# Last feed-forward stage: the weights' high part meets both halves of x in one 512-column matmul

## The chip, the core and the metric

The kernel runs on one core of a Trainium2 chip. Its engines are TensorE (PE, with its weight loads shown as PEld), VectorE (DVE), ScalarE (ACT), GpSimd (POOL) and SyncE (SP), which issues the transfers. The metric is the device time of one execution in microseconds (us), lower is better.

## The reference

Two blocks of two layers each follow each other on a sequence of 256 tokens of width 1024. The first block has three kinds of attention and a mixture of experts, the second puts 16 meta tokens in front (272 in all) and has a delta-rule mixer in its first layer, dense attention in its second, each with a feed-forward after it. The change is in the very last feed-forward:

```python
u = rmsnorm(h, mlp_norm_g[layer])
h = h + jnp.square(jax.nn.relu(u @ w_ff1[layer])) @ w_ff2[layer]
return h[:, N_META:]
```

`w_ff1` is 1024 x 4096, `w_ff2` 4096 x 1024. Everything is float32. In this last layer the meta tokens are no longer needed, so the stage works on 256 columns (tokens), the same stage of the layer before on 272.

## The kernel before

**Numbers in two parts.** PE multiplies in a fast format (fp32r) that keeps fewer bits, so each operand a is split into a high part, a rounded to that format, and a low part, a - high. `wsplit` (lines 256 and 267 for the subtraction) splits 128 x 1024 weights: ACT converts the high part (line 236, out `ring`), DVE subtracts (line 267). `split` does the same for a result (ACT, then DVE at line 249). `mm3` forms a product as three matmuls into one bank: high weights with high x (line 272), high weights with low x (273), low weights with high x (274). Each matmul instruction has its own weight load. `form_a` does this for the eight slices of 128 of a contraction of 1024, one slice being called a k-step here: 24 matmuls per block of 128 output features.

**The stage.** `mlp(l, lo, out)` is called with `lo=16` for the last layer, so n = 256. Its input u is h2 times the norm's gain, in two parts; the norm's factor per token (`rs`) is put on the way out of the first product. The hidden width of 4096 is worked through in four quarters. In each, ff1 makes eight blocks: 24 matmuls into a bank, then on DVE `max(b, 0) * rs` into `fr` (line 245), its square on POOL (line 1299), and the split into rh (ACT) and rl (DVE). Then ff2 makes eight blocks of the 1024 output features from the quarter's rh and rl, the first two of them side by side k-step by k-step, and DVE adds each to the residual h2 (`add_h`, line 1269). In the last quarter `leave` sends two features blocks of h2 out at a time. So the stage has 32 blocks of ff1 and 32 of ff2.

**What sets the order.** The tile framework turns the program into one queue per engine and puts in the semaphores; each engine then works through its queue in order, and that order need not be the one in which the code writes the instructions. Split weights lie in two pairs of buffers in turn (`NW = 2`), so the split of block i+2 may begin when block i has been multiplied; the second block of the side-by-side pair takes a ring slot instead (`spare`). There are four banks for such products, and two buffers each of rh, rl and fr. Weights come in from SP's queue in transfers of 1 MB into ring slots. `norm_start(i, lo)` prepares u for the next stage one feature block at a time as h2 gets its last addend: ACT writes uh, DVE ul (line 245), ACT and POOL sum the squares; i = 3 is the norm ahead of this stage, called by the output projection of the attention (`out_proj`).

Of the kernel before, what the change touches and what calls it, by code (L numbers as in the profile page):

```python
# [10 lines left out]
F32R = mybir.dt.float32r  # L11
# [14 lines left out]
N2 = S + 16  # L26
# [154 lines left out]
class Kern:  # L181
# [11 lines left out]
    def bank(self, tag="bank"):  # L193
        return self.ps.tile([128, 512], F32, name=tag, bufs=BANKS[tag])
# [1026 lines left out]
    def hcols(self, t):  # L1221
        return slice(0, 16) if t == 0 else slice(16 + 128 * (t - 1), 144 + 128 * (t - 1))

    def norm_tiles(self, n):

        uh, ul = (self.hp.tile([128, 8, N2], F32R, name=m)[:, :, :n] for m in ("uh", "ul"))
        acc = self.hp.tile([128, N2], F32, name="acc")[:, :n]

        def scale():
            ss = self.aux()[:, :n]  # L1230
            self.nc.tensor.matmul(ss, self.ones, acc, start=True, stop=True)
            rs = self.hp.tile([128, N2], F32, name="nrs")[:, :n]
            self.rstd(rs, ss, D, self.eps6)
            return rs

        self.norm = (uh, ul), scale
        return uh, ul, acc

    def square(self, acc, x, k):
# [5 lines left out]
            self.nc.gpsimd.tensor_add(acc, acc, sq)  # L1245

    def norm_start(self, i, lo=0):
        uh, ul, acc = self.norm_tiles(N2 - lo)

        def step(k):  # L1250
            x, g = self.h2[:, k, lo:], self.g2[:, i, k:k + 1]
            self.act(uh[:, k], x, AF.Copy, scale=g)
            self.stt(ul[:, k], x, g, uh[:, k].bitcast(F32), OP.mult, OP.subtract)
            self.square(acc, x, k)

        return step
# [10 lines left out]
    def add_h(self, k, b, lo=0, then=None):  # L1267
        n = N2 - lo
        self.nc.vector.tensor_add(self.h2[:, k, lo:], self.h2[:, k, lo:], b[:, :n])  # L1269
        if then is not None:  # L1270
            then(k)

    def mlp(self, l, lo=0, out=None):
        nc, a, tc = self.nc, self.a, self.tc
        n = N2 - lo
        then = None

        def leave(k):
            if k % 2:
                nc.sync.dma_start(out[:, k - 1:k + 1], self.h2[:, k - 1:k + 1, 16:])  # L1280

        with ExitStack() as c:
            p2 = c.enter_context(tc.tile_pool(name=f"Fw{l}", bufs=2))
            u, scale = self.norm
            rs = None
            for q in range(4):
                rh = p2.tile([128, 8, n], F32R, name="rh")
                rl = p2.tile([128, 8, n], F32R, name="rl")
                for c4 in range(2):
                    w = self.ring(a["w_ff1"][l, 2 * q + c4])  # L1290
                    for j in range(4):
                        f = 4 * c4 + j
                        b = self.bank()[:, :n]
                        self.form_a(b, w[:, j * 1024:(j + 1) * 1024], u)
                        if rs is None:
                            rs = scale()
                        r = p2.tile([128, n], F32, name="fr")
                        self.stt(r, b, 0.0, rs, OP.max, OP.mult)
                        nc.gpsimd.tensor_mul(r, r, r)  # L1299
                        self.split(rh[:, f], rl[:, f], r)  # L1300
                if q == 3:
                    then = self.norm_start(2) if out is None else leave
                for c4 in range(2):
                    w = self.ring(a["w_ff2"][l, 2 * q + c4])
                    pair = range(0 if c4 else 2)
                    if pair:
                        bs = [self.bank()[:, :n] for _ in pair]
                        parts = [self.wsplit(w[:, j * 1024:(j + 1) * 1024], spare=j == 1) for j in pair]
                        for k in range(8):
                            c = slice(k * 128, (k + 1) * 128)  # L1310
                            for b, (hi, lw) in zip(bs, parts):
                                self.mm3(b, (hi[:, c], lw[:, c]), (rh[:, k], rl[:, k]), k == 0, k == 7)
                        for j, b in enumerate(bs):
                            self.add_h(j, b, lo, then)
                    for j in range(len(pair), 4):
                        f = 4 * c4 + j
                        b = self.bank()[:, :n]
                        self.form_a(b, w[:, j * 1024:(j + 1) * 1024], (rh, rl))
                        self.add_h(f, b, lo, then)

    def conv_silu(self, p, b, rs, wc, out):

# [1027 lines left out]
```

## Time and profile before

| | |
|---|---|
| Median of three runs | 1559.42 us (1555.83 to 1578.79) |
| Profiled execution | 1559.64 us |
| Its span in the profile | 1557.9 us |
| PE, DVE, ACT, POOL busy | 95%, 53%, 41%, 11% of the span |
| First matmul of the changed stage | 1369.87 us |
| Last matmul's end | 1554.06 us |

A profile row gives an instruction's start and its duration in us, the engine, the source line, the operation, the tiles it writes and reads (out<-in), their shapes, and how many were merged; in brackets the engine's idle time before it and what ended that. Matmuls overlap: a row's duration holds the time until its results are out, and the distance from one start to the next is what a matmul takes of PE.

### The profile page before, as it was taken

To read this page: it belongs to the slowest core of one execution; us is meant where nothing else is said; L and a number is where in the kernel's file an instruction comes from. 1 tells how busy PE (TensorE), PEld (TensorE's weight loads), DVE (VectorE), ACT (ScalarE), POOL (GpSimd) and SP (SyncE) were. 2 spreads that over 40 slices of the span, in tenths; PEclk is the share of its full clock that TensorE was granted. 3 is DMA by queue.
4 is the path that set the end of the run, shared out by engine and by line. 5 is a ranking of instruction groups with operands and counts; after the bars stand their busy time and mean duration, and the time that the engine had idled before them with its cause. 6 is when DMAs were issued, how large, how long until landed. Compare 5 with 4: busy or idle time off the path is not lost.

```text
span 1557.9 us, 26416 instructions
## 1 busy us (share of the span) xinstructions
PE 1479.8 (95%) x10806; PEld 1128.8 (72%) x10806; DVE 821.7 (53%) x1594; ACT 638.1 (41%) x1265; POOL 178.2 (11%) x226
## 2 busy tenths in 40 slices
PE   8999999999799999999989888899999999999999
PEld 7888744344388874434328777679999997899998
DVE  6687712212336782222126686557556566576665
ACT  5466411111246642111125674455444455554443
POOL 0130000000001000000003530302001123221000
PEclk9999999999899999999998998799999999999999
DMA  9336799999833679999943210036454542255540
GB/s 382 121 136 222 300 417 420 383 421 423 331 134 108 222 300 391 422 383 421 422 193 120 71 54 31 1 136 243 163 184 168 190 145 84 83 196 185 179 141 28
DMA packets 50033, 348.76 MB, mean 224 GB/s; under 512 B 5616, under 2 KB 6896, under 8 KB 8688
## 3 DMA queue, kind: packets, MB, share of 16 engines
q1 hardware_dynamic: 49904, 346.97, 57.9%
q8 instruction: 89, 1.46, 0.4%
q14 instruction: 40, 0.33, 0.1%
HBM read 345.90 MB, written 1.05 MB: 223 GB/s over the span
## 4 chain that ended last, share of the span: by engine, by line
PE 43%; DVE 5%; ACT 3%; POOL 1%; issue 1%; DVEq 0%; POOLq 0%; ACTq 0%
PE bank L274 10%; PE bank L272 10%; PE bank L273 10%; PE bank L1060 3%; PE bank L1102 2%; DVE ring L267 1%; PE aux L297 1%; ACT ring L236 1%; PE aux L2059 1%; PE bank L1690 1%; PE aux L1558 1%; PE aux L2037 1%; POOL cy L1336 0%; DVE v L245 0%; PE bank L1847 0%
## 5 line engine op out<-in xcount | busy, mean ns | idle before, releaser
L236 ACT ACTIVATE ring<-ring 128x1024 fp32r<-128x1024 f32 (+4 forms) x198 | 196.2, 1001 | 211.1 <-PE bank L274 189.4
L267 DVE TENSOR_TENSOR ring<-ring,ring 128x1024 fp32r<-128x1024 f32 x162 | 202.8, 1253 | 93.8 <-ACT ring L236 93.5
L274 PE MATMUL bank<-uh,ring 128*128 128x272 f32 (+1 forms) x744 | 216.9, 292 | 7.4 <-DVE ring L267 6.0
L272 PE MATMUL bank<-uh,ring 128*128 128x272 f32 (+1 forms) x744 | 220.0, 296 | 3.3 <-ACT ring L236 3.3
L273 PE MATMUL bank<-ul,ring 128*128 128x272 f32 (+1 forms) x744 | 215.8, 290 | 0.0
L274 PEld LDWEIGHTS bank<-uh,ring 128*128 128x128 f32 x744 | 142.9, 192 | 9.4 <-DVE ring L267 7.5
L272 PEld LDWEIGHTS bank<-uh,ring 128*128 128x128 f32 x744 | 142.8, 192 | 5.4 <-ACT ring L236 4.2
L273 PEld LDWEIGHTS bank<-ul,ring 128*128 128x128 f32 x744 | 142.6, 192 | 0.6
L274 PE MATMUL bank<-rh,ring 128*128 128x272 f32 (+1 forms) x496 | 141.7, 286 | 0.0
L272 PE MATMUL bank<-rh,ring 128*128 128x272 f32 (+1 forms) x496 | 141.5, 285 | 0.0
L273 PE MATMUL bank<-rl,ring 128*128 128x272 f32 (+1 forms) x496 | 140.9, 284 | 0.0
L1073 DVE TENSOR_TENSOR hid<-hid,bank 128x512 f32<-128x512 f32 x16 | 11.0, 687 | 193.4 <-PE bank L1060 193.4
L273 PEld LDWEIGHTS bank<-rl,ring 128*128 128x128 f32 x496 | 93.8, 189 | 0.0
L272 PEld LDWEIGHTS bank<-rh,ring 128*128 128x128 f32 x496 | 93.2, 188 | 0.0
L274 PEld LDWEIGHTS bank<-rh,ring 128*128 128x128 f32 x496 | 93.0, 188 | 0.0
L245 DVE SCALAR_TENSOR_TENSOR big<-bank,gs,big 128x512 fp32r<-128x512 f32 x32 | 24.0, 751 | 108.8 <-ACT big L236 107.3
L1299 POOL TENSOR_TENSOR fr<-fr 128x272 f32<-128x272 f32 (+1 forms) x64 | 40.0, 627 | 287.5 <-DVE fr L245 283.6
L236 ACT ACTIVATE big<-bank,gs 128x512 fp32r<-128x512 f32 x32 | 22.0, 687 | 102.2 <-PE bank L1102 101.9
L1269 DVE TENSOR_TENSOR h<-h,bank 128x272 f32<-128x272 f32 (+1 forms) x80 | 33.2, 426 | 51.5 <-PE bank L274 51.5
L236 ACT ACTIVATE hid<-bank 128x512 f32<-128x512 f32 x24 | 14.3, 597 | 108.9 <-PE bank L1060 103.9
L1083 ACT COPY hidT<-bank 128x512 f32<-128x512 f32 x16 | 9.4, 586 | 118.3 <-PE bank L297 118.3
L1102 PE MATMUL bank<-big,hidT 128*64 128x512 f32 x208 | 47.8, 595 | 0.1
(668 smaller groups left out, 3391.4 us busy)
## 6 DMA issues: line engine op xcount, KB each, us to landing
ring<-w_ff SPq DMA_DIRECT2D x58, 1024.0 KB, 4.8
big<-w_gate SPq DMA_DIRECT2D x30, 1024.0 KB, 17.5
big<-w_up SPq DMA_DIRECT2D x29, 1024.0 KB, 18.1
big<-w_down SPq DMA_DIRECT2D x26, 1024.0 KB, 17.1
ring<-w_gate SPq DMA_DIRECT2D x24, 1024.0 KB, 14.1
ring<-w_down SPq DMA_DIRECT2D x24, 1024.0 KB, 17.5
ring<-w_up SPq DMA_DIRECT2D x20, 1024.0 KB, 18.1
big<-w_in SPq DMA_DIRECT2D x9, 1024.0 KB, 11.8
```

The costliest lines, as they stand in the source:

```text
L236: return self.nc.scalar.activation(out, in_, func, **kw)
L245: return (eng or self.nc.vector).scalar_tensor_tensor(out, in0, s, in1, op0=op0, op1=op1, **kw)
L267: (eng or self.nc.vector).tensor_sub(l, src, h.bitcast(F32))
L272: mm(out, lhs[0], rhs[0], start=first, stop=False)
L273: mm(out, lhs[0], rhs[1], start=False, stop=False)
L274: mm(out, lhs[1], rhs[0], start=False, stop=last)
L297: self.nc.tensor.transpose(out, in_, self.ident[:k, :k])
L1060: mm(b[e * 64:e * 64 + CAP], xg[:, k, e * CAP:(e + 1) * CAP], w[:, (2 * k + e) * 512:(2 * k + e + 1) * 512], start=k == 0, stop=k == 7)
L1102: mm(yb[n][e * 64:e * 64 + CAP], hT[:, k, e * 64:e * 64 + CAP], w[:, o:o + 512], start=k == 0, stop=k == 3)
L1269: self.nc.vector.tensor_add(self.h2[:, k, lo:], self.h2[:, k, lo:], b[:, :n])
L1299: nc.gpsimd.tensor_mul(r, r, r)
L1558: nc.tensor.matmul(ob[r, dst.start - c0:dst.stop - c0], vba[:n, u, r], x[:n, u], start=u == 0, stop=u == 2)
```

## The change

Where n is 256, u lies in one tile `uw` with both parts of a k-step side by side (256 columns high, 256 low), and so do rh and rl. A whole bank of 512 columns takes a block. A k-step is two matmuls: the high weights with all 512 columns, the low weights with the 256 high ones, into the bank's first half. The last k-step has them the other way round. On the way out the two halves are summed: in ff1 ACT copies the second half into `fr` and DVE adds the first half to it, after which `max` and `rs` are applied to `fr` in place; in ff2 DVE adds first one half and then the other to h2. The stage of 272 columns keeps the three matmuls.

```diff
--- before.py
+++ after.py
@@ -1221,9 +1221,13 @@
     def hcols(self, t):
         return slice(0, 16) if t == 0 else slice(16 + 128 * (t - 1), 144 + 128 * (t - 1))
 
-    def norm_tiles(self, n):
-
-        uh, ul = (self.hp.tile([128, 8, N2], F32R, name=m)[:, :, :n] for m in ("uh", "ul"))
+    def norm_tiles(self, n, wide=False):
+
+        if wide:
+            u = self.hp.tile([128, 8, 2, n], F32R, name="uw")
+            uh, ul = u[:, :, 0], u[:, :, 1]
+        else:
+            u = uh, ul = [self.hp.tile([128, 8, N2], F32R, name=m)[:, :, :n] for m in ("uh", "ul")]
         acc = self.hp.tile([128, N2], F32, name="acc")[:, :n]
 
         def scale():
@@ -1233,7 +1237,7 @@
             self.rstd(rs, ss, D, self.eps6)
             return rs
 
-        self.norm = (uh, ul), scale
+        self.norm = u, scale
         return uh, ul, acc
 
     def square(self, acc, x, k):
@@ -1245,7 +1249,7 @@
             self.nc.gpsimd.tensor_add(acc, acc, sq)
 
     def norm_start(self, i, lo=0):
-        uh, ul, acc = self.norm_tiles(N2 - lo)
+        uh, ul, acc = self.norm_tiles(N2 - lo, i == 3)
 
         def step(k):
             x, g = self.h2[:, k, lo:], self.g2[:, i, k:k + 1]
@@ -1270,31 +1274,66 @@
         if then is not None:
             then(k)
 
+    def wide(self, out, parts, x, k, first, last):
+
+        hi, lo = parts
+        c = slice(k * 128, (k + 1) * 128)
+        steps = [(out, hi[:, c], x[:, k]), (out[:, 0], lo[:, c], x[:, k, 0])]
+        for o, w, m in steps[::-1] if last else steps:
+            self.nc.tensor.matmul(o, w, m, start=first and o is out, stop=last and o is out)
+
     def mlp(self, l, lo=0, out=None):
         nc, a, tc = self.nc, self.a, self.tc
         n = N2 - lo
         then = None
+        both = n == 256
 
         def leave(k):
             if k % 2:
                 nc.sync.dma_start(out[:, k - 1:k + 1], self.h2[:, k - 1:k + 1, 16:])
+
+        def bank():
+            return self.bank().rearrange("p (a s) -> p a s", a=2) if both else self.bank()[:, :n]
+
+        def block(b, parts, x, k):
+            if both:
+                return self.wide(b, parts, x, k, k == 0, k == 7)
+            c = slice(k * 128, (k + 1) * 128)
+            self.mm3(b, (parts[0][:, c], parts[1][:, c]), (x[0][:, k], x[1][:, k]), k == 0, k == 7)
+
+        def add(f, b):
+            if both:
+                nc.vector.tensor_add(self.h2[:, f, lo:], self.h2[:, f, lo:], b[:, 1])
+                b = b[:, 0]
+            self.add_h(f, b, lo, then)
 
         with ExitStack() as c:
             p2 = c.enter_context(tc.tile_pool(name=f"Fw{l}", bufs=2))
             u, scale = self.norm
             rs = None
             for q in range(4):
-                rh = p2.tile([128, 8, n], F32R, name="rh")
-                rl = p2.tile([128, 8, n], F32R, name="rl")
+                if both:
+                    rt = p2.tile([128, 8, 2, n], F32R, name="rh")
+                    rh, rl = rt[:, :, 0], rt[:, :, 1]
+                else:
+                    rh = p2.tile([128, 8, n], F32R, name="rh")
+                    rl = p2.tile([128, 8, n], F32R, name="rl")
+                    rt = rh, rl
                 for c4 in range(2):
                     w = self.ring(a["w_ff1"][l, 2 * q + c4])
                     for j in range(4):
                         f = 4 * c4 + j
-                        b = self.bank()[:, :n]
-                        self.form_a(b, w[:, j * 1024:(j + 1) * 1024], u)
+                        b = bank()
+                        parts = self.wsplit(w[:, j * 1024:(j + 1) * 1024])
+                        for k in range(8):
+                            block(b, parts, u, k)
                         if rs is None:
                             rs = scale()
                         r = p2.tile([128, n], F32, name="fr")
+                        if both:
+                            nc.scalar.copy(r, b[:, 1])
+                            nc.vector.tensor_add(r, r, b[:, 0])
+                            b = r
                         self.stt(r, b, 0.0, rs, OP.max, OP.mult)
                         nc.gpsimd.tensor_mul(r, r, r)
                         self.split(rh[:, f], rl[:, f], r)
@@ -1304,19 +1343,19 @@
                     w = self.ring(a["w_ff2"][l, 2 * q + c4])
                     pair = range(0 if c4 else 2)
                     if pair:
-                        bs = [self.bank()[:, :n] for _ in pair]
+                        bs = [bank() for _ in pair]
                         parts = [self.wsplit(w[:, j * 1024:(j + 1) * 1024], spare=j == 1) for j in pair]
                         for k in range(8):
-                            c = slice(k * 128, (k + 1) * 128)
-                            for b, (hi, lw) in zip(bs, parts):
-                                self.mm3(b, (hi[:, c], lw[:, c]), (rh[:, k], rl[:, k]), k == 0, k == 7)
+                            for b, p in zip(bs, parts):
+                                block(b, p, rt, k)
                         for j, b in enumerate(bs):
-                            self.add_h(j, b, lo, then)
+                            add(j, b)
                     for j in range(len(pair), 4):
-                        f = 4 * c4 + j
-                        b = self.bank()[:, :n]
-                        self.form_a(b, w[:, j * 1024:(j + 1) * 1024], (rh, rl))
-                        self.add_h(f, b, lo, then)
+                        b = bank()
+                        parts = self.wsplit(w[:, j * 1024:(j + 1) * 1024])
+                        for k in range(8):
+                            block(b, parts, rt, k)
+                        add(4 * c4 + j, b)
 
     def conv_silu(self, p, b, rs, wc, out):
 
```

## Rows read from the trace of the kernel before

**Rows 1.** The page, part 1: busy time, share of the span, instructions.

```profile
PE 1479.8 (95%) x10806; PEld 1128.8 (72%) x10806; DVE 821.7 (53%) x1594; ACT 638.1 (41%) x1265; POOL 178.2 (11%) x226
```

**Rows 2.** Busy by stretch: us, PE, PEld, DVE, ACT, POOL (counts), PEclk, DMA share, GB/s.

```profile
1369.90:1554.10 184.20, 183.75 (x1540) 183.29 (x1538) 114.44 (x161) 80.00 (x98) 20.96 (x34) 1.00 0.41 142
...
1416.70:1439.50 22.80, 22.80 (x195) 22.80 (x194) 15.54 (x23) 11.42 (x15) 4.30 (x7) 1.00 0.55 186
```

**Rows 3.** The chain of waits, stage alone, by line.

```profile
by line: PE bank L274 32.3%; PE bank L273 32.0%; PE bank L272 31.8%; ACT ring L236 0.6%; POOL acc L1245 0.5%; PE aux L1231 0.4%; DVE h L1269 0.2%; ACT uh L236 0.2%; ACT nsq L236 0.2%; issue 0.1%; POOLq L1245 0.0%
```

**Rows 4.** Groups of instructions in the stage: busy us, mean ns | idle before.

```profile
L267 DVE TENSOR_TENSOR ring<-ring,ring 128x1024 fp32r<-128x1024 f32 x55 | 67.6, 1230 | 34.9 <-ACT ring L236 34.9
...
L245 DVE SCALAR_TENSOR_TENSOR fr<-bank,nrs 128x256 f32<-128x256 f32 x32 | 13.6, 424 | 6.2 <-PE bank L274 6.1
```

**Rows 5.** PE in order of time: first matmuls of ff1, ff2, next ff1.

```profile
1416.72 0.28 PE L272 MATMUL bank<-uh,ring 128*128 128x256 f32 x1
...
1439.41 0.28 PE L272 MATMUL bank<-rh,ring 128*128 128x256 f32 x1
...
1462.45 0.28 PE L272 MATMUL bank<-uh,ring 128*128 128x256 f32 x1
```

**Rows 6.** PE in order of time: 512-column matmuls, long run, then mixed.

```profile
148.00 0.39 PE L273 MATMUL bank<-wsp,ring 128*128 128x512 f32 x1
...
153.90 0.39 PE L272 MATMUL aux<-ring,ring 128*128 128x512 f32 x1
...
161.69 0.40 PE L272 MATMUL bank<-wsp,big 128*128 128x512 f32 x1
...
162.16 0.28 PE L273 MATMUL aux<-big,ring 128*16 128x256 f32 x1
```

**Rows 7.** PE in order of time: 272-column matmuls of the earlier stage.

```profile
1170.08 0.29 PE L272 MATMUL bank<-uh,ring 128*128 128x272 f32 x1
...
1179.92 0.29 PE L272 MATMUL bank<-uh,ring 128*128 128x272 f32 x1
```

**Rows 8.** One ff1 block's way out, by engine in order of time.

```profile
1419.52 0.28 PE L272 MATMUL bank<-uh,ring 128*128 128x256 f32 x1
...
1422.48 0.19 PEld L274 LDWEIGHTS bank<-uh,ring 128*128 128x128 f32 x1
...
1422.60 0.28 PE L274 MATMUL bank<-uh,ring 128*128 128x256 f32 x1
...
1419.72 1.06 ACT L236 ACTIVATE ring<-ring 128x1024 fp32r<-128x1024 f32 x1 [1.74 <-PE bank L274]
1420.93 0.42 ACT L236 ACTIVATE rh<-fr 128x256 fp32r<-128x256 f32 x1 [0.15 <-POOL fr L1299]
...
1419.72 0.42 DVE L245 SCALAR_TENSOR_TENSOR fr<-bank,nrs 128x256 f32<-128x256 f32 x1 [0.48 <-PE bank L274]
1420.81 1.22 DVE L267 TENSOR_TENSOR ring<-ring,ring 128x1024 fp32r<-128x1024 f32 x1 [0.67 <-ACT ring L236]
```

**Rows 9.** ACT copies out of a bank; DVE line 245 with SBUF operands.

```profile
1298.03 0.35 ACT L2052 COPY PTc<-aux 128x256 f32<-128x256 f32 x1
1298.28 0.25 ACT L2053 COPY PTc<-aux 16x128 f32<-16x128 f32 x1
...
1296.78 0.48 DVE L245 SCALAR_TENSOR_TENSOR crx<-cub,wsp,csq 128x256 f32<-128x256 f32 x1 [0.33 <-ACT csq L236]
...
1364.89 0.96 DVE L245 SCALAR_TENSOR_TENSOR ul<-h,wsp,uh 128x256 fp32r<-128x256 f32 x1
```

**Rows 10.** The first block's last k-step: DVE and PE.

```profile
1372.30 0.95 DVE L245 SCALAR_TENSOR_TENSOR ul<-h,wsp,uh 128x256 fp32r<-128x256 f32 x1
1372.34 0.28 PE L272 MATMUL bank<-uh,ring 128*128 128x256 f32 x1
```

**Rows 11.** DVE adds to h2: after a pair, and at the end.

```profile
1399.28 0.78 DVE L1269 TENSOR_TENSOR h<-h,bank 128x256 f32<-128x256 f32 x2 [2.75 <-PE bank L274]
...
1554.09 0.42 DVE L1269 TENSOR_TENSOR h<-h,bank 128x256 f32<-128x256 f32 x1 [2.45 <-PE bank L274]
```

## The prediction

> **What bounds the kernel now.** I read the page's busy shares first: PE is busy for 95% of the span [rows 1]. Then the stretches of the stage that the change touches, the last feed-forward (1369.9 to 1554.1 us): in the 22.8 us from 1416.7, which are the first half of one quarter, PE and its weight loads are both busy without a gap, the granted clock is 1.00 (the 2.4 GHz level), DVE is busy 15.54 us of 22.8, ACT 11.42 [rows 2]. The chain of waits through the stage agrees: 96% of it is lines 272 to 274, the three matmuls of a k-step [rows 3]. So the stage is a stream of matmuls, and its time is their number times the distance from one start to the next. The duration that a matmul's row shows (0.28) is longer than that distance and is not what one costs.
>
> The distance is read from starts. In the first half of a quarter (ff1) 192 matmuls of 256 columns lie between 1416.72 and 1439.41: 22.69 / 192 = 118.2 ns each. In the second half (ff2), 192 from there to 1462.45: 23.04 / 192 = 120.0 ns [rows 5]. At 2.4 GHz 256 columns stream in 106.7 ns, so each matmul costs 11.5 or 13.3 ns beside its columns. Is that a price per matmul or per column? A run of 512-column matmuls in the same number format has 26 steps from 148.00 to 153.90: 226.9 ns, 13.6 over the 213.3 of its columns [rows 6]. A run of 272 columns has 78 steps from 1170.08 to 1179.92: 126.2 ns, 12.8 over 113.3 [rows 7]. Twice the columns, the same surplus: it belongs to the matmul. This is what the change can save, and nearly all of it, because the number of columns streamed (768 per k-step) stays.
>
> **The change part by part.**
> *Products.* Of three matmuls per k-step (256 columns each) remain one of 512 and one of 256. There are 64 blocks of 8 k-steps. ff1: before 3 x 118.2 = 354.6 ns, after 226.9 + 118.2 = 345.1, saved 9.5. ff2: before 360.0, after 226.9 + 120.0 = 346.9, saved 13.1. The first ff1 block gains nothing: PE reaches its last k-step at 1372.34 and waits there for ul, which DVE ends at 1373.25 [rows 10], and the changed order waits for the same ul. So 31 x 8 x 9.5 ns = 2.4 us and 32 x 8 x 13.1 ns = 3.4 us: 5.8 us saved.
> No row shows 512 and 256 columns in turn with weights that change each time. From below: no surplus is left, 320 ns per k-step, which saves 34.6 x 248 + 40 x 256 = 8.6 + 10.2 = 18.8 us. From above: in a mixed stretch two 512-column matmuls took 235 ns each (161.69 to 162.16 for both) [rows 6], so 353.2 and 355.0 per k-step, which saves 1.4 x 248 + 5 x 256 = 1.6 us. I take the long run's 226.9, since it is 26 alike in the same place of a queue, and the mixed stretch has other products between.
>
> *Way out of ff1.* New per block: an ACT copy of the low half, a DVE add of the two halves, and the max-times-scale that reads SBUF now. DVE per block was 1.23 (low part of the weights), 0.42 and 0.42; it becomes some 2.5 us of a block of 8 x 345.1 = 2.76 us [rows 4], ACT some 1.9 (1.06, 0.42 and the new 0.36). Neither is the bound by its sum, but the order in the queues matters. Two weight pairs alternate: the high part of block i+2 can be converted on ACT only when block i has left PE, and DVE subtracts after that. Now ACT starts this conversion at 1419.72, DVE the subtraction at 1420.81 until 1422.03 [rows 8], that is 2.31 after the block's visible end T. When it is needed: the next block's first matmul starts 0.20 before T (1419.52); the block after that starts 2.76 later, its first low-part matmul 0.23 on, and that one's weight load 0.12 earlier (1422.48 against 1422.60): T + 2.67 [rows 8].
> With the change ACT gets the copy at T too. It is earlier in the program, so I expect it first. From a like copy to the next ACT start there are 0.25 us [rows 9], so the conversion runs from T + 0.27 to 1.33. DVE meanwhile adds (T + 0.39, next start 0.35 later) and scales (from 0.74); the scaling with SBUF operands took 0.48, or 0.96 beside a POOL instruction [rows 9], and POOL's square comes after it. So it is done before the subtraction, which runs from T + 1.36 to 2.58. Margin 0.06 us (it was about 0.5). I cost this way out at nothing: PE's stream hides it. If the cover is gone by x, that is lost once per two blocks (two pairs): at 0.40 for the copy, x = 0.09 and 32 x 0.045 = 1.4 us. The bound below is nothing gained, since PE did not wait there.
> Behind the copy ACT also queues the conversion of the squared result, behind the add DVE queues the rest of that block's split. Who waits for these is ff2, a k-step of which reads one feature block; the last of them is read at the end of the first pair, some 5 us later.
>
> *Way out of ff2.* A second DVE add per block (0.42, second of two 0.36 later [rows 11]). It fills the 0.67 that DVE waits for ACT ahead of a subtraction [rows 8]: the adds end at T + 0.78, the subtraction starts at T + 1.09. After the pair of blocks there are four adds instead of two, T to T + 1.44, then the subtraction to 2.66: due at 2.67 again, so nothing. At the end of the kernel nothing hides it: the last add ends at 1554.51 now [rows 11], one more costs 0.36 us, before the last output transfer.
>
> *The rest.* The normalised input lands in one fresh tile instead of two reused ones, the instructions are the same and none waits longer. The weight transfers are issued by the same rule at the same places; DMA share in the stage is 0.41 [rows 2] and the stage wants its weights 3% faster. The last k-step puts the low-part matmul ahead of the wide one, which changes no count. The other feed-forward (272 columns) takes the old path.
>
> Sum against the profiled execution of 1559.64 (span 1557.9 and 1.74 around it): 1559.64 - 5.8 + 0.36 = 1554.2 us. The median of the three runs is 1559.42, 0.2 lower, so it stands for both.
>
> [...]
>
> **The rivals.**
> A, weight loads set the pace. Loads are busy the whole stage [rows 2], and one of three goes. If the surplus comes from loads that don't quite fit beside 256 columns, under 512 they fit, and the k-step falls towards 320 ns: 1559.64 - 18.8 + 0.36 = 1541.2. Against it: 512 columns leave room for a load of 0.19 and still show 13.6 ns of surplus [rows 6]. [...]
> B, the other side: the subtraction falls behind the way out. Place: DVE's queue in each of 32 ff1 blocks. If ACT converts the weights first and copies after (T + 0.97 to 1.33) and DVE's queue has the add and the scaling ahead of the subtraction, it runs from 2.13 to 3.35, is seen at 3.38 and due at 2.67: 0.71 per two blocks, 32 x 0.355 = 11.4 us. 1554.2 + 11.4 = 1565.6, slower than before; it decides against the change once the delay passes 5.4 us / 16 = 0.34 per two blocks. For it: DVE's queue is in a fixed order, and the trace already has ACT instructions ahead of ones that the code writes earlier (the weights of block i+2 before the result of block i [rows 8]). Against it: that reordering favours the weights, on DVE too.
> C, the change doesn't do what it says: the wide matmul costs what the mixed stretch shows (235 ns). Saved 1.6, less 0.36: 1558.4. For it: only that stretch has changing shapes. Against it: its neighbours differ in output and weights' width too.
>
> **How the numbers follow.** Forecast 0.62 (own range 1552.5 to 1556.5: the copy's 1.4 us upward, 11.5 instead of 13.6 ns for ff1's wide matmul downward), A 0.10, B 0.13, C 0.15. The range 1546 to 1566 holds the forecast, C, B and the halfway part of A; what is left out is A's end, and a B with a larger delay. A change of 2% (31 us) is about what a measurement of this kernel tells from none. No case reaches 1528, since 768 columns stream in 320 ns: 0.01 for what I can't see. Slower than 1591 would need three times B's delay: 0.04. Within 2%: 0.95.
>
> **What would show it.** PE matmuls in the stage fall from 1536 to 1024, starts of a k-step are 345 to 347 ns apart, and the weight loads' busy share falls below 1. The chain stays on PE. ACT's row order in an ff1 block is copy, weights, result, and DVE's subtraction ends about 2.6 us after the block. Waits of PE on the ring's DVE subtraction, some tenths each in ff1, would show B; k-steps of 320 ns A; of 353 C. The forecast is wrong in its main step if 227 + 119 isn't what wide and narrow cost in turn.

## The result, and the profile after

The changed kernel takes 1575.59 us in the median of 22 runs (1569.41 to 1594.18), the kernel before 1563.28 in 22 runs beside it. The ratio is 1.0074, with a 95% interval of 1.0062 to 1.0087: slower by 12 us, where 5 us less were forecast. It lies within the 2% that counted as the same, and above the range given. One run of the 22, the longest, had a lower granted clock (0.92 for 0.97) and is left out of the ratio.

The profiled execution took 1577.20 us, 17.6 more than that of before. 5.0 of these lie ahead of the stage: its first matmul starts at 1374.87 instead of 1369.87. Five kernels of the experiments, whose code ahead of the stage is the changed one's, start it anywhere from 1370.30 to 1374.45, so this is a difference between executions. The stage itself, from there to the end of the last add, went from 184.64 us (1369.87 to 1554.51) to 196.89 (1374.87 to 1571.76): 12.25 more, the same as the medians say. All readings below are of the stage.

The page of the kernel after, part 1, as in [rows 1]:

```profile
PE 1488.2 (94%) x10294; PEld 1101.6 (70%) x10294; DVE 847.8 (54%) x1658; ACT 644.1 (41%) x1297; POOL 207.3 (13%) x226
```

The matmuls fell by 512, as the change says. POOL has as many instructions as before, 226, and yet is busy for 29 us more (178.2 in [rows 1]). That is the first thing to follow up: an engine whose work was not changed. The busy shares by stretch, after, the whole stage and then six ff1 blocks of one quarter (columns as in [rows 2]):

```profile
1374.90:1571.80 196.90, 187.68 (x1028) 154.84 (x1026) 140.85 (x225) 85.91 (x130) 50.50 (x34) 1.00 0.38 133
...
1428.00:1448.40 20.40, 18.85 (x102) 14.84 (x101) 14.37 (x24) 9.83 (x19) 9.43 (x6) 1.00 0.46 160
```

POOL's time in the stage rose from 20.96 us [rows 2] to 50.50 for the same 34 instructions. PE, which had no gap in the stretch of [rows 2], stands still here for 1.55 of 20.40 us (by its rows, which hold the time until results are out; by starts it is more, see below). The clock is 1.00 in both. Groups of instructions in the stage, after:

```profile
L267 DVE TENSOR_TENSOR ring<-ring,ring 128x1024 fp32r<-128x1024 f32 x57 | 70.2, 1231 | 4.4 <-ACT ring L236 4.0
...
L1338 POOL TENSOR_TENSOR fr<-fr 128x256 f32<-128x256 f32 x32 | 49.2, 1536 | 125.0 <-ACT ring L236 72.1 <-DVE fr L245 52.9
```

The square of the ff1 result, the one thing that POOL does per block, takes 1536 ns in place of 614; this is its group in the stage before:

```profile
L1299 POOL TENSOR_TENSOR fr<-fr 128x256 f32<-128x256 f32 x32 | 19.6, 614 | 139.7 <-DVE fr L245 135.7 <-PE bank L274 3.9
```

Why it does is seen in order of time. Timeline of the kernel after, merged from the engines: the first ff1 block's square and the subtraction beside it, then one later block in full, with the two matmul streams that start when a subtraction is done.

```profile
1380.71 0.61 POOL L1338 TENSOR_TENSOR fr<-fr 128x256 f32<-128x256 f32 x1 [2.73 <-DVE fr L245]
1380.80 1.60 DVE L267 TENSOR_TENSOR ring<-ring,ring 128x1024 fp32r<-128x1024 f32 x1 [0.24 <-ACT ring L236]
...
1430.96 0.35 ACT L1334 COPY fr<-bank 128x256 f32<-128x256 f32 x1
1431.08 0.42 DVE L249 TENSOR_TENSOR rh<-fr,rh 128x256 fp32r<-128x256 f32 x1 [0.95 <-ACT rh L236]
1431.21 1.06 ACT L236 ACTIVATE ring<-ring 128x1024 fp32r<-128x1024 f32 x1
1431.43 0.41 DVE L1335 TENSOR_TENSOR fr<-fr,bank 128x256 f32<-128x256 f32 x1
1431.88 0.42 DVE L245 SCALAR_TENSOR_TENSOR fr<-fr,nrs 128x256 f32<-128x256 f32 x1
1432.31 1.23 DVE L267 TENSOR_TENSOR ring<-ring,ring 128x1024 fp32r<-128x1024 f32 x1
1432.44 1.56 POOL L1338 TENSOR_TENSOR fr<-fr 128x256 f32<-128x256 f32 x1 [1.84 <-DVE fr L245]
1433.59 3.07 PE L1283 MATMUL bank<-uw,ring 128*128 128x256 f32 x16 [0.24 <-DVE ring L267]
1434.04 0.42 ACT L236 ACTIVATE rh<-fr 128x256 fp32r<-128x256 f32 x1 [1.76 <-POOL fr L1338]
1434.36 0.36 ACT L1334 COPY fr<-bank 128x256 f32<-128x256 f32 x1
...
1436.99 1.32 PE L1283 MATMUL bank<-uw,ring 128*128 128x256 f32 x6 [0.33 <-DVE ring L267]
```

ACT's and DVE's queues run in the forecast order: copy, weights' high part, result's high part; add, scaling, subtraction. Counted from the copy at 1430.96 the subtraction starts 1.35 later, where 1.36 was forecast. Two things were not forecast. The copy itself is late: its block's last matmul had ended at 1430.31, and ACT first had to do the high part of the block before, which had waited for POOL's square (one block on, the lag from the last matmul's end, 1433.12, to the copy, 1434.36, is 1.24 us). And DVE now goes from the scaling straight into the subtraction (1432.31), and POOL's square, released by the same scaling, starts 0.13 later. It ends 0.46 after the subtraction does: of its usual 0.61 it got done only some 0.15 in the 1.10 us for which both ran. In the first block POOL was 0.09 ahead, and there it is DVE's subtraction that took 1.60 for 1.23. Before, 0.67 us of waiting for ACT lay between scaling and subtraction [rows 8], and the square ran in this gap:

```profile
1420.29 0.61 POOL L1299 TENSOR_TENSOR fr<-fr 128x256 f32<-128x256 f32 x1 [25.23 <-DVE fr L245]
...
1423.13 0.62 POOL L1299 TENSOR_TENSOR fr<-fr 128x256 f32<-128x256 f32 x1 [2.23 <-DVE fr L245]
```

It ended at 1420.90, 0.09 after the subtraction had begun at 1420.81 [rows 8]. Once in the stage before, the square started some 0.3 us late and the two did meet, and there the later one, the subtraction, took 1.46 for 1.22:

```profile
1529.08 0.61 POOL L1299 TENSOR_TENSOR fr<-fr 128x256 f32<-128x256 f32 x1 [2.51 <-DVE fr L245]
1529.31 1.46 DVE L267 TENSOR_TENSOR ring<-ring,ring 128x1024 fp32r<-128x1024 f32 x1 [0.67 <-ACT ring L236]
```

The distance of the two squares' starts at 1420.29 and 1423.13, 2.84 us, is the block of before. After, it is 3.40 (1430.96 to 1434.36 from copy to copy on ACT, 1433.59 to 1436.99 on PE). The chain of waits, after, shows what sets the 3.40; first its shares in the whole stage, then in 11 us of ff1 (a step that reaches over an end of these 11 us counts whole, so the shares add up to more than 100%), then the steps of one block:

```profile
by line: PE bank L1283 45.1%; POOL fr L1338 18.1%; DVE fr L245 5.2%; DVE rh L249 5.1%; DVE ring L267 5.0%; ACT rh L236 4.9%; DVE fr L1335 4.1%; issue 3.5%; ACT ring L236 2.6%; DVE wsp L256 1.2%; DVE h L1306 0.9%; DVE ring L256 0.6%; POOL ac
...
by line: POOL fr L1338 57.7%; ACT rh L236 15.5%; DVE fr L245 11.9%; DVE rh L249 11.6%; DVE fr L1335 9.3%; issue 5.3%; POOLq L1338 0.5%
...
1432.44 1.57 POOL fr L1338
...
1434.04 0.43 ACT rh L236
...
1434.49 0.43 DVE rh L249
1434.91 0.34 DVE fr L1335
...
1435.28 0.43 DVE fr L245
...
1435.85 1.57 POOL fr L1338
```

PE had 96% of the stage's chain [rows 3] and has 45% now; in those 11 us of ff1 it is not in it at all. The loop reads: the square (1.57), the high part of the squared result on ACT (0.43), its low part on DVE (0.43), and behind that, because DVE's queue is in a fixed order, the next block's add (0.34) and scaling (0.43), which release the next square. With the small gaps that is 3.41 us, and PE's block would take 2.81 (the first experiment). A second way round is hardly shorter: on ACT the next block's copy stands behind that same high part, and it leads to the same add. PE itself sees the loop as a wait for the subtraction, which each round of the loop releases; waits of its weight loads in the stage, after (engine, line, waited for: us in total, times, longest):

```profile
PEld bank L1283 <- DVE ring L267: 19.4, 27, 0.9
```

A quarter has seven such distances from its first square to its eighth: 23.87 us (1428.97 to 1452.84) where it was 19.88 (1420.29 to 1440.17), 4.0 lost. From there to the next quarter's first square it is 24.99 (to 1477.83) where it was 25.85 (to 1466.02), 0.9 given back. That is 3.1 us a quarter and 12.5 in four, close to the 12.25 measured over the whole stage.

### The profile page after: what moved, and what is told of

Its sections match the earlier page's. It is cut to its first block, busy times and chain, and to the rows that moved or that the text cites. A ratio compares the mean times of both kernels' runs of the same rounds, so it can differ in the third digit from the quotient of the medians.

```text
span 1575.0 us, 25495 instructions
## 1 busy us (share of the span) xinstructions
PE 1488.2 (94%) x10294; PEld 1101.6 (70%) x10294; DVE 847.8 (54%) x1658; ACT 644.1 (41%) x1297; POOL 207.3 (13%) x226
## 4 chain that ended last, share of the span: by engine, by line
PE 37%; DVE 7%; POOL 4%; ACT 4%; issue 2%; DMA 1%; POOLq 0%; ACTq 0%; DVEq 0%
PE bank L274 6%; PE bank L1283 6%; PE bank L272 6%; PE bank L273 6%; PE bank L1060 3%; POOL fr L1338 2%; PE bank L1102 2%; DVE ring L267 1%; ACT ring L236 1%; PE aux L297 1%; PE aux L2098 1%; PE aux L1597 1%; POOL cy L1375 1%; DVE fr L245 1%; DVE rh L249 1%
## 5 line engine op out<-in xcount | busy, mean ns | idle before, releaser
L272 PE MATMUL bank<-uh,ring 128*128 128x272 f32 (+1 forms) x488 | 147.4, 302 | 4.9 <-ACT ring L236 3.3
L274 PE MATMUL bank<-uh,ring 128*128 128x272 f32 (+1 forms) x488 | 143.8, 295 | 6.8 <-DVE ring L267 6.8
L273 PE MATMUL bank<-ul,ring 128*128 128x272 f32 (+1 forms) x488 | 142.6, 292 | 0.0
L1283 PE MATMUL bank<-uw,ring 128*128 128x512 f32 (+1 forms) x512 | 96.1, 341 | 6.0 <-DVE ring L267 6.0
L274 PEld LDWEIGHTS bank<-uh,ring 128*128 128x128 f32 x488 | 93.4, 191 | 8.7 <-DVE ring L267 8.4
L272 PEld LDWEIGHTS bank<-uh,ring 128*128 128x128 f32 x488 | 93.4, 191 | 7.3 <-ACT ring L236 4.2
L1283 PEld LDWEIGHTS bank<-uw,ring 128*128 128x128 f32 x512 | 77.1, 188 | 24.4 <-DVE ring L267 14.6
L273 PEld LDWEIGHTS bank<-ul,ring 128*128 128x128 f32 x488 | 93.5, 192 | 0.6
L1283 PE MATMUL bank<-rh,ring 128*128 128x512 f32 x480 | 89.4, 338 | 1.8 <-DVE ring L267 1.8
L1283 PEld LDWEIGHTS bank<-rh,ring 128*128 128x128 f32 x480 | 73.4, 188 | 15.2 <-DVE ring L267 4.9
L274 PE MATMUL bank<-rh,ring 128*128 128x272 f32 x256 | 73.8, 288 | 0.0
L272 PE MATMUL bank<-rh,ring 128*128 128x272 f32 x256 | 73.7, 288 | 0.0
L273 PE MATMUL bank<-rl,ring 128*128 128x272 f32 x256 | 73.6, 287 | 0.0
```

The costliest lines, as they stand in the source:

```text
L272: mm(out, lhs[0], rhs[0], start=first, stop=False)
L273: mm(out, lhs[0], rhs[1], start=False, stop=False)
L274: mm(out, lhs[1], rhs[0], start=False, stop=last)
L1283: self.nc.tensor.matmul(o, w, m, start=first and o is out, stop=last and o is out)
```

## The experiments

Seven kernels were run. "Stage" is the time from its first matmul to the end of its last add: 184.64 us before, 196.89 after. Each time and ratio below is of 12 runs, where no other number is given; each stage is of one profiled execution. The kernel before, run beside them, took 1561.19 us (29 runs, beside the square on ACT, the wide product in one half alone and the later split) and 1563.18 (23 runs, beside the control and the two kernels with another order of products).

**The square on ACT, the change otherwise whole.** The theory: the square beside the subtraction, and nothing else of the way out, costs the time.

```diff
-                        nc.gpsimd.tensor_mul(r, r, r)
+                        if both:
+                            self.act(r, r, AF.Square)
+                        else:
+                            nc.gpsimd.tensor_mul(r, r, r)
```

> The changed kernel with ff1's square on ACT (Square) instead of POOL, nothing else. Lengths are from the stage's first matmul to the issue of the last output transfer: 184.7 us before, 196.9 after the change. Theory (square and weight subtraction collide: POOL's square takes 1.57 instead of 0.61 beside DVE's subtraction, and it lies in a loop square, high part, low part, next block's add, scaling, next square of 3.40 us per ff1 block): the square takes about 0.4, the loop falls below a block's matmuls, an ff1 block takes about 2.8 us, the stage 182 us, 0.998 of before. Rival 1 (DVE's queue: the subtraction stands behind add and scaling and is late whatever POOL does): an ff1 block stays at 3.4, the stage near 197, 1.007. Rival 2 (ACT's queue: the new copy holds up the weights' high part): ACT gets more work, the stage is 197 or longer.

1562.59 us, ratio to before 1.0006 (0.9983 to 1.0030), stage 183.67 (1374.45 to 1558.12). Timeline of ACT in this kernel, one ff1 block and the next one's copy:

```profile
1424.31 0.37 ACT L1334 COPY fr<-bank 128x256 f32<-128x256 f32 x1 [1.75 <-PE bank L1283]
1424.58 1.06 ACT L236 ACTIVATE ring<-ring 128x1024 fp32r<-128x1024 f32 x1
1425.63 0.42 ACT L236 ACTIVATE fr<-fr 128x256 f32<-128x256 f32 x1
1426.08 0.42 ACT L236 ACTIVATE rh<-fr 128x256 fp32r<-128x256 f32 x1
1427.12 0.37 ACT L1334 COPY fr<-bank 128x256 f32<-128x256 f32 x1 [0.62 <-PE bank L1283]
```

The square at 1425.63 takes 0.42 beside a subtraction that starts at 1425.67 and takes 1.23: ACT and DVE don't hold each other up here. The block falls to 2.81 us, ACT waits for PE again, and 13.2 of the stage's 196.89 us go. So the square beside the subtraction is where the loss comes from, and both rivals stated for this run fall. What is left of the change, 184.64 - 183.67 = 1.0 us, is less than these runs can tell from nothing; a stage of 182 was expected, 1.7 shorter.

**The same square on ACT in the kernel before**, as a control: is ACT simply the better place?

```diff
-                        nc.gpsimd.tensor_mul(r, r, r)
+                        if n == 256:
+                            self.act(r, r, AF.Square)
+                        else:
+                            nc.gpsimd.tensor_mul(r, r, r)
```

> The kernel before with the square of the last stage on ACT, its products unchanged. Theory: POOL's square took 0.61 there and met no one, so nothing changes: stage 184.6, ratio 1.000. If this is faster or slower by more than its interval, the square's engine matters by itself and e1_square_act has to be read against it.

1562.01 us, ratio 1.0007 (0.9982 to 1.0032), stage 184.65 (1372.10 to 1556.75). It makes no difference where square and subtraction do not meet (but for the one time shown above), so the 13 us above are not a gain of ACT's.

**The wide product in ff2 alone, and in ff1 alone.** One kernel keeps the three narrow matmuls and the old way out in ff1, the other in ff2.

```diff
...
-                        b = bank()
-                        parts = self.wsplit(w[:, j * 1024:(j + 1) * 1024])
-                        for k in range(8):
-                            block(b, parts, u, k)
+                        b = self.bank()[:, :n]
+                        self.form_a(b, w[:, j * 1024:(j + 1) * 1024], u)
...
-                        if both:
-                            nc.scalar.copy(r, b[:, 1])
-                            nc.vector.tensor_add(r, r, b[:, 0])
-                            b = r
```

> The wide product in ff2 alone; ff1 has its three products and its way out of before. Theory: an ff2 block takes 2.81 instead of 2.88 us, 32 x 0.075 = 2.4 us less, 0.45 more for the last add: stage 182.7 us, ratio 0.9988. Rival 3 (the wide matmul itself is what costs): no gain or slower, stage 185 or more, and then the loss isn't only ff1's.

1562.42 us, ratio 1.0003 (0.9983 to 1.0022), stage 184.34 (1371.30 to 1555.64): a gain of 0.3 us where about 2 were expected. That alone is near the 185 of rival 3, the wide matmul as the cost. What speaks against it is ff2 by quarters, from its first matmul to the next ff1's: 22.98, 22.95 and 22.95 us where it was 23.04 each, and in the fourth, to its last matmul's end, 22.63 where it was 23.20. The wide matmul saves; what eats the gain in three quarters is shown further down, behind the pair.

```diff
...
-                            add(j, b)
+                            self.add_h(j, b, lo, then)
...
-                        b = bank()
-                        parts = self.wsplit(w[:, j * 1024:(j + 1) * 1024])
-                        for k in range(8):
-                            block(b, parts, rt, k)
-                        add(4 * c4 + j, b)
+                        b = self.bank()[:, :n]
+                        self.form_a(b, w[:, j * 1024:(j + 1) * 1024], (rh, rl))
+                        self.add_h(4 * c4 + j, b, lo, then)
```

> The wide product in ff1 alone; ff2 has its three products and one add. Theory: all of the loss is ff1's and ff2 gave back 2: stage 196.9 + 2 = 199 us, an ff1 block 3.40, an ff2 block 2.88. Rival 3 (the wide matmul itself costs): the loss is split between both halves, the stage near 191.

A single run: 1575.09 us, so without an interval; stage 197.18 (1372.81 to 1569.99), expected 199. Its square, in the groups of the stage:

```profile
L1338 POOL TENSOR_TENSOR fr<-fr 128x256 f32<-128x256 f32 x32 | 49.1, 1534 | 125.3 <-ACT ring L236 70.5 <-DVE fr L245 54.8
```

With ff2 as before the square still takes 1534 ns and the ff1 block 3.40. The whole loss is ff1's; the two halves (-0.3 and +12.5 us) add up to the change's 12.25.

**The split of the squared result one block later in both queues**, so that the square is no longer between one block's add and the next one's: the collision stays, the loop is cut.

```diff
...
-                        self.split(rh[:, f], rl[:, f], r)
+                        if both:
+                            late.append((rh[:, f], rl[:, f], r))
+                            if len(late) > 1:
+                                with tc.issue_after(copied.ins), tc.issue_after(scaled.ins):
+                                    self.split(*late.pop(0))
```

(`copied` and `scaled` are the block's copy and scaling; `fr` has three buffers.)

> The changed kernel with the split of a squared result (high part on ACT, low part on DVE) queued one block later: behind the next block's copy on ACT and behind the next block's scaling on DVE; fr has three buffers. The square stays on POOL and still meets the subtraction. Theory: POOL's square still takes about 1.5 us, but it is no longer in a loop with the next block's add; the weights' high part now stands behind copy and result's high part, the subtraction is 0.25 late per two blocks: an ff1 block takes 2.9 us, the stage 185 to 186, 1.000 to 1.001 of before. Rival 1: add and scaling are still ahead of the subtraction, and one more instruction too, so an ff1 block takes 3.4 or more, the stage 197 or more.

1566.15 us, ratio 1.0034 (1.0016 to 1.0052), stage 190.05 (1370.30 to 1560.35). About half of the loss went, less than expected. Timeline, POOL and DVE of one block, then ACT's copies of three:

```profile
1429.05 0.67 POOL L1339 TENSOR_TENSOR fr<-fr 128x256 f32<-128x256 f32 x1 [2.14 <-DVE fr L245]
1429.30 1.50 DVE L267 TENSOR_TENSOR ring<-ring,ring 128x1024 fp32r<-128x1024 f32 x1
...
1427.62 0.37 ACT L1335 COPY fr<-bank 128x256 f32<-128x256 f32 x1 [1.14 <-PE bank L1283]
1430.92 0.37 ACT L1335 COPY fr<-bank 128x256 f32<-128x256 f32 x1 [1.66 <-PE bank L1283]
1433.73 0.37 ACT L1335 COPY fr<-bank 128x256 f32<-128x256 f32 x1 [1.16 <-PE bank L1283]
```

The expectation had POOL pay the collision as before. It doesn't: the delayed split sits between scaling and subtraction on DVE, so the square starts 0.25 ahead, takes 0.67, and the subtraction takes 1.50. Whichever starts second pays. The subtraction in turn is what PE waits for, and blocks alternate between 3.30 and 2.81, which fits two pairs of weights in turn. So 0.49 us per two blocks remain: 0.27 of it is the longer subtraction, 1.50 for 1.23, and the rest is about the 0.25 that was expected of ACT's queue, where the weights' high part now stands behind that of the result.

**Other order of the products.** The sixteen matmuls of a block go wide for k = 0 to 6, narrow for k = 0 to 7, wide for k = 7, so that the low weights are first needed later in the block. Once with POOL's square, once with ACT's.

```diff
-        steps = [(out, hi[:, c], x[:, k]), (out[:, 0], lo[:, c], x[:, k, 0])]
-        for o, w, m in steps[::-1] if last else steps:
-            self.nc.tensor.matmul(o, w, m, start=first and o is out, stop=last and o is out)
+        for i in range(16):
+            high = i < 7 or i == 15
+            k = 7 if i == 15 else i if high else i - 7
+            c = slice(k * 128, (k + 1) * 128)
+            for out, (hi, lo) in pairs:
+                if high:
+                    self.nc.tensor.matmul(out, hi[:, c], x[:, k], start=i == 0, stop=i == 15)
+                else:
+                    self.nc.tensor.matmul(out[:, 0], lo[:, c], x[:, k, 0], start=False, stop=False)
...
```

> The changed kernel with the matmuls of a block in another order: seven wide ones, all eight narrow ones, the last wide one. The weights' low part, which DVE's subtraction makes, is then wanted 1.6 us later in the block. The square stays on POOL. Theory (the loop square, high part, low part, next add, scaling sets 3.40 us whatever PE does): an ff1 block stays at 3.40 us, the stage at 195 (only the waits of 0.5 us per quarter behind ff2's pair go). Rival 1 (the subtraction comes too late for PE, by 0.3 us per ff1 block): it is in time now, an ff1 block takes 2.8 us, the stage 182.

With POOL's square: 1573.86 us (4 runs), ratio 1.0090 (1.0063 to 1.0116), stage 195.36 (1370.65 to 1566.01), about the 195 of the theory. Waits in its stage:

```profile
ACT rh L236 <- POOL fr L1343: 55.5, 32, 2.0
...
PEld bank L1285 <- ACT ring L236: 9.8, 16, 0.7
```

PE no longer waits for DVE's subtraction, for which it had waited in the kernel after; it waits for ACT's high part of the weights instead, and the block is 3.40 as before (two squares start at 1427.72 and 1431.12). So PE's wait for the subtraction was where the loss was seen, not its cause: take it away and the loop shows up at the next wait.

> The order of e5_grouped and the square on ACT as in e1_square_act (stage 183.7 there, a k-step of 0.350 us, waits of 0.46 us per quarter behind ff2's pair). Theory: the waits behind the pair go (1.8 us less). If wide and narrow matmuls cost more in turn than in runs (0.350 against 0.2269 + 0.118), a k-step falls to 0.345 and a block to 2.76: stage 179; if not, blocks stay at 2.80 and the stage is 182. Either is shorter than the 184.6 before: ratio 0.997 or 0.9985.

With ACT's square: 1562.37 us, ratio 1.0000 (0.9982 to 1.0018), stage 183.08 (1373.90 to 1556.98); of the two figures expected, 179 and 182, the higher was nearer and still too low. Its order has runs of equal shapes, which gives the price of each in this stage. PE in order of time:

```profile
1422.82 2.03 PE L1285 MATMUL bank<-uw,ring 128*128 128x512 f32 x8
1424.68 1.12 PE L1287 MATMUL bank<-uw,ring 128*128 128x256 f32 x8
1425.64 2.03 PE L1285 MATMUL bank<-uw,ring 128*128 128x512 f32 x8
```

Eight wide ones take 1424.68 - 1422.82 = 1.86 us, 232.5 ns each; eight narrow ones 0.96 us, 120 each. Together 352.5 per k-step, against 354.6 and 360.0 before [rows 5]. The gain over before, 1.6 us in the stage, is too small for these runs to tell.

**Behind the pair.** The kernel with ACT's square shows what is left of the way out of ff2. Its DVE after a pair, in order of time:

```profile
1449.29 0.78 DVE L1306 TENSOR_TENSOR h<-h,bank 128x256 f32<-128x256 f32 x2 [2.36 <-PE bank L1283]
1449.98 0.74 DVE L1273 TENSOR_TENSOR h<-h,bank 128x256 f32<-128x256 f32 x2
1450.64 1.22 DVE L267 TENSOR_TENSOR ring<-ring,ring 128x1024 fp32r<-128x1024 f32 x1
1452.45 0.42 DVE L1306 TENSOR_TENSOR h<-h,bank 128x256 f32<-128x256 f32 x1 [0.59 <-PE bank L1283]
1452.91 0.42 DVE L1273 TENSOR_TENSOR h<-h,bank 128x256 f32<-128x256 f32 x1
1453.24 1.22 DVE L256 TENSOR_TENSOR ring<-ring,ring 128x1024 fp32r<-128x1024 f32 x1
1454.38 1.22 DVE L267 TENSOR_TENSOR ring<-ring,ring 128x1024 fp32r<-128x1024 f32 x1
1455.52 0.41 DVE L1306 TENSOR_TENSOR h<-h,bank 128x256 f32<-128x256 f32 x1
```

The first subtraction starts 1.35 after the first add, near the forecast 1.44. But two more follow, one of them for the next quarter's pair (line 256), and DVE has no gap from 1452.45 on. The next blocks come out 3.16, 3.07 and 3.01 us apart. The 3.16 is as it should be, since the first block of the pair is done one k-step (0.35) ahead of the second; the other two are 0.26 and 0.20 over 2.81, 0.46 us per quarter. The fourth quarter has no next pair to prepare, line 256 is not in its queue, and its blocks stay at 2.81, so three quarters lose 1.4 us together. In this kernel PE waits for a subtraction once more, at the stage's start: the first matmuls of the third and fourth ff1 block lie 3.14 us apart (1381.19 to 1384.33), 0.33 over 2.81. The kernel with ff2 alone wide shows the same two distances, 3.07 and 3.01. In the reordered kernel with ACT's square, where the low weights are due later in a block, DVE is late too, but the adds come 3.07, 3.06 and 2.59 us apart: it catches up, and PE loses nothing.

## Why the prediction was wrong, and where it was right

**"So it is done before the subtraction", and with it "I cost this way out at nothing".** This is the step that failed. The text followed DVE's scaling past POOL's square and had the subtraction at T + 1.36, which is where it is, counted from the copy. By its own figures the scaling ended at about T + 1.2, so the square, 0.61 long, had to run into the subtraction; it never put the two beside each other. The row that shows what happens then was even read: line 245 with SBUF operands, 0.48 alone and 0.96 beside a POOL instruction [rows 9], which had started 0.07 ahead of it (1364.82). It was applied to the scaling alone. Before the change the square had ended 0.09 us after the subtraction began.

**"Who waits for these is ff2 ... some 5 us later."** Also wrong, and it turned a late square into a lower pace. The rest of the split waits for the square, it stands in DVE's queue ahead of the next block's add, and the add leads to the next square. A loop through three engines does not care how late ff2 needs its result: 3.40 us per block against some 2.8. The margins were all counted from the block's end T, and the loop moved the copy, which starts the way out, 0.6 to 1.3 us behind that in the quarter shown. The run with the split moved cut the loop and took 6.8 of the 12.25 us away; the run with the square on ACT took the rest too.

**The saving of 5.8 us.** The mechanism holds: matmuls cost a fixed surplus each and fewer of them cost less. The wide one was mis-sized, "the long run's 226.9" where this stage has 232.5; the 235 of the mixed stretch [rows 6], taken as the far end, was the nearer. In the alternating order of the change, with the square on ACT, a k-step takes about 350.7 ns in both halves (three ff1 blocks in 8.42 us, an ff2 block in 2.805). That saves 248 x 3.9 + 256 x 9.3 = 3.3 us, not 5.8 (5.7, before its two terms were rounded). The forecast's own range, 1552.5 to 1556.5, was wider than the two reasons given for it make it, 1553.7 to 1555.6. Why the same instruction costs 227 in one place and 232 here is open; no run varied it alone.

**"Due at 2.67 again, so nothing", behind the pair.** Wrong by 1.4 us, in three of the four quarters: it followed one subtraction after the four adds and not the two behind it, the spare pair's among them. The late subtraction at the stage's start, 0.3 us, was not seen either. The last add was right: 0.42 to 0.46 us more at the end for 0.36 forecast.

Without the collision the sum would so have been -3.3 + 1.4 + 0.3 + 0.4 = -1.2 us; the stage with the square on ACT measured -1.0. So the forecast of 5 us less would have failed without the collision too: that kernel's ratio, 0.9983 at the least, allows for 2.7.

**The rivals.** A fell: with the weight loads' busy time down from 183.29 us [rows 2] to 154.84 no k-step came near 320 ns. C, with the price of the mixed stretch (353.2 and 355.0 ns), was nearer to the 350.7 than the forecast (345.1 and 346.9) in ff1 and about as far off in ff2; the 3.3 us saved lie between its 1.6 and the forecast's 5.8. B was nearest in time (1565.6; its delay of 11.4 us stands beside the 13.2 that the square on ACT gave back) and named the place, DVE's subtraction in ff1, and the sign that PE waits for it (27 waits of its weight loads in the kernel after, 0.72 us each in the mean); but of its mechanism only DVE's part, add and scaling ahead of the subtraction, occurred, and that was in the forecast too; ACT didn't convert the weights ahead of the copy. The rival that happened, two engines in each other's way, was not in the list.

## What to carry to other kernels

When a change closes a gap in one engine's queue, look at what another engine did in that gap: here a wait of 0.67 us on DVE was the place in which POOL's square ran undisturbed, and the change filled it. Where an operation's result comes back to its own issuer through a fixed queue, add up the loop, and compare it with the block; a margin on each due time is not enough. A product saved is worth its measured surplus in that very stage, some 4 to 9 ns of a k-step of 355 to 360 here, and not the columns or the weight loads that it appears to free.

## What was not expected of the hardware

In these runs POOL and DVE hardly overlapped when both read their operands in SBUF. A 128 x 256 square on POOL took 0.61 us alone and 1.56 when started 0.13 us after DVE's 128 x 1024 subtraction, which kept its 1.23. With POOL ahead by 0.09 or 0.25 us the square took 0.61 or 0.67 and the subtraction 1.60 or 1.50. The one that starts second does little until the other is done: each time it got through some 0.15 us of its work in the 0.4 to 1.1 us for which both ran. The Trainium skill bears on this: GPSIMD Engine Reference, section Key points, says that GpSimd shares its interfaces to SBUF with VectorE and contends with VectorE's instructions that have two SBUF inputs. The subtraction is one, and the trace agrees; that the loser is the later of the two is from these runs. No run changed where an operand of these two lies. But the kernel before has, in an earlier stage, a DVE product of 128 x 272 with one operand in a bank and the other in SBUF, beside a POOL addition:

```profile
875.79 0.44 DVE L1416 TENSOR_TENSOR qw<-bank,nrs 128x272 f32<-128x272 f32 x1 [0.69 <-PE bank L274]
875.81 0.78 POOL L1336 TENSOR_TENSOR cy<-cy,tap 128x272 f32<-128x272 f32 x1
```

Neither is longer than elsewhere: the same addition at 868.16, with DVE idle, took 0.77, and the other such products 0.43 to 0.44. So it isn't any work on DVE that holds POOL up. That the same square on ACT takes 0.42 us beside an undisturbed subtraction fits too. That the shared interface is the cause is argued from these rows and not tested by a change of its own.
